# Branch B's inverse rms by halves of the queries, with the pieces of the phases set anew

## The chip, the cores and the metric

The kernel runs on one core of a Trainium2 chip. The metric is the device time of one execution in microseconds; lower is better. Engines are called as in the profile: PE (TensorE, matmuls), PEld (its weight loads), DVE (VectorE), ACT (ScalarE), POOL (GpSimd) and SP (SyncE, which here issues every DMA).

## The reference

One encoder layer is applied to two request groups ("prompt" and "sample") of 1024 tokens and 1024 channels that share the weights. Everything is float32. For the change, branch B matters: four heads, each with two softmax maps whose difference weighs 128-dimensional values, then an rms norm over each head's 128 values, a gate, and a projection.

```
qb = rms_norm(qb.reshape(B, S, H_B, 2, HEAD_DIM), qn_b)
kb = rms_norm(kb.reshape(B, S, H_B, 2, HEAD_DIM), kn_b)
...
ob = diff_attention(qb, kb, vb, lam)            # (p0 - lam * p1) @ v for each head
ob = rms_norm(ob, subln_g) * (1.0 - lam_init)
ob = ob.reshape(B, S, BR_B) * jax.nn.silu(zb)

pa = jnp.einsum('bse,ed->bsd', oa, w_proj_a)
pb = jnp.einsum('bse,ed->bsd', ob, w_proj_b)
merged = jax.nn.sigmoid(ga) * pa + jax.nn.sigmoid(gb) * pb
out = jnp.einsum('bsd,de->bse', merged, w_out)
return x + gate[:, None, :] * out
```

Branch A is grouped-query attention with 8 query heads; its output `oa` is gated in the same way, without the norm over the head.

## The kernel before, in words

The two groups go one after the other through the same stages: a head (projection of keys and values and of the first queries), attention of branch A in phases 0 and 1 (32 units), attention of branch B in phases 2 to 5 (one phase for each head, four units of 256 queries each, `pr` 0 to 3), the gating and the merge of both branches (lines 1028 to 1109), and the output projection (L1128). Matmuls mostly split each float32 operand into a high and a low part and add three products; that is why each block comes as hh, hl and lh.

**Order.** The kernel is written with a tile framework. Python generators emit the work step by step, and `weave` (line 82) interleaves them: each stream has a number of steps and a lead, and the stream that is least far along, less its lead, goes next. `Z_SHARE`, `ATT_W`, `IN_A`, `Z_A`, `LAST_ATT`, `GATED_A`, `FIRST_A` and the like are these numbers and leads for each group and phase. `BEHIND` says how many units the value matmuls of a branch B unit come after its scores; `A_WAIT` how many steps a branch A unit waits ahead of its values. What is emitted first has priority, attention steps more (`AHEAD`, `TRAIN`); a planner then puts each engine's instructions in one fixed order by when its model of time says that they are ready and have a buffer. So on the chip each engine runs its list in order, and the list is not the order of the code.

**Buffers around the change.** PSUM has three "f" banks (projections, merge sums, transposes, the sums of squares of line 975), two "s" tiles (attention scores; after attention also merge sums, `gbank`), and one "a" bank (values). In SBUF the tag "tab" has two buffers, "row" three, "q" two.

**The inverse rms of branch B.** `b_values` (line 937) ends a unit: the value matmuls (L953) fill the a bank; ACT squares it (L968), DVE copies it out (L969), SP sends it to DRAM (L971, `od`); two small matmul pairs against a column of ones sum the squares of 256 queries (L975); DVE copies the two columns into `ss`, a tile of 128 partitions by 4 heads by 8 query tiles (L977). After the last unit of a head (`pr == 3`) POOL computes, over all 8 columns, `(ss + su * su * 2 * HD * EPS) ** -0.5` (L980 to L983); `su` is the first softmax's sum, by which the values have not been divided.

`gated_gen(st, i, hf, oT)` (line 1028) makes the gated inputs of the merge: `i` is a pair of 128-channel blocks (0 and 1 are branch A, 2 and 3 are heads 0, 1 and 2, 3 of branch B), `hf` one half of the queries (512). For `i > 1` and `hf == 0` it transposes the inverse rms of both heads and all queries on PE (L1041, 128x16), copies it out on ACT (L1043) and sends it to DRAM in one write (L1044). Then for each half and each of the two blocks it reads the output and the gate (L1055, L1056) and the row of inverse rms, spread over 128 partitions (L1063), multiplies (L1064, L1068 on DVE) and splits the product into its high part (L1069, ACT) and low part (L1070, DVE).

`merge_gen` (line 1075) multiplies these with the projection weights (L1097): sixteen sums of 12 matmuls for branch A, then sixteen for branch B, in the order of half of the output, half of the queries, block. Of the 12, six take block pair 2 and six pair 3. DVE takes the sums out with the gates (L1108 for A; L1103, L1104, L1106 for B, with ACT at L1105).

In the last attention phase `weave` mixes attention, `fill` (what is left of the gate projections, then 14 or 11 merge sums of branch A) and the gating of pairs 0 to 2; then come the rest of merge A with pair 3's first half, and merge B with its second half.

The code of the functions that the change touches, with the profile's line numbers:

Of the kernel before, what the change touches and what calls it, by code (L numbers as in the profile page):

```python
# [12 lines left out]
F32 = mybir.dt.float32  # L13
# [7 lines left out]
P = 128  # L21
# [3 lines left out]
NTT = T // P  # L25
# [10 lines left out]

Z_SHARE = (
    (8, 21, 4, 2, 4, 3),
    (13, 12, 5, 3, 2, 6),
)  # L40
Z_HEAD = (7, 6)
Z_HEAD_A = (-0.3, -0.32)
ATT_W = (
    (0.825, 1.067, 1.068, 1.192, 1.03, 1.769),
    (1.154, 1.862, 1.041, 1.271, 0.783, 1.144),
)
IN_A = (
    (0.32, -0.07, 0.7, 0.05, 0.25, 0.15),
    (0.1, -0.05, 0.33, 0.3, -0.03, 0.55),
)  # L50
Z_A = (
    (0.2, 0.05, 0.12, -0.05, -0.1, -0.05),
    (0.03, 0.07, 0.2, 0.15, -0.3, -0.1),
)
LAST_ATT = (47, 41)
LAST_FILL = (22, 23)
GATED_A = (0.1, -0.15)
LATE_A = 0.95
QUARTER_P = 200
KV_STEPS = 12  # L60
GATE_AT = 9
FIRST_ATT = 15
FIRST_A = 0.26
TAIL = (2, 5)
TAIL_A = (1.15, 1.2)
LAG = 2
Z_FIRST = (9, 8)
Z_FIRST_A = (-0.05, -0.05)

CUTS = (3, 6)  # L70

BEHIND = 1.4
BEHIND_A = 1.4
AHEAD = 100
PV_LAG = 2
A_WAIT = 1
TRAIN = 200

WHOLE = (True, True)
# [31 lines left out]
def kernel(ctx: ExitStack, tc: tile.TileContext, t: dict):  # L111
# [825 lines left out]
    def b_values(u):  # L937
        acc = ps_a.tile([P, 512], F32, tag="a", name=nm("a"))[:, :256]
        ready = []
        def pv(cc, th, tl):  # L940
            for c in range(2):
                k = cc * 2 + c
                for s, rt in ((0, th), (0, tl), (1, th)):
                    nc.tensor.matmul(
                        acc, u["v"][:, k, s, :], rt[:, c, :],
                        start=(k == 0 and s == 0 and rt is th), stop=(k == 7 and s == 1),
                    )

        if WHOLE[u["h"] // 2]:
            pT = u["pT"].bitcast(F32).rearrange("p (q c b) -> p c q b", q=8, c=8)  # L950
            yield 1
            for k in range(NCH):
                nc.tensor.matmul(acc, u["v"][:, k], pT[:, k], start=(k == 0), stop=(k == 7))  # L953
                if k % 2:
                    yield 1
        else:
            for piece in pT_pieces(u):
                ready.append(piece)
                if len(ready) > PV_LAG:
                    pv(*ready.pop(0))  # L960
                yield 1
            while len(ready) > 1:
                pv(*ready.pop(0))
                yield 1
            pv(*ready.pop())
        sq = mtile("at", [P, 256], bufs=1)
        o = mtile("oo", [P, 256])
        nc.scalar.activation(query_order(sq), piece_order(acc), AF.Square)  # L968
        nc.vector.tensor_copy(query_order(o), piece_order(acc))  # L969
        pr = u["pr"]  # L970
        dma(u["od"][pr // 2][:, (pr % 2) * 256 : (pr % 2 + 1) * 256], o)  # L971
        yield 1
        ps = fbank()
        for i in range(2):
            nc.tensor.matmul(ps[:, i : i + 1], sq[:, i * P : (i + 1) * P], ones_c, start=True, stop=True)  # L975
        ss = u["ss"][:, u["h"]]
        nc.vector.tensor_copy(ss[:, pr * 2 : pr * 2 + 2], ps[:, 0:2])  # L977
        if pr == 3:
            su = u["su"]
            nc.gpsimd.tensor_tensor(out=su, in0=su, in1=su, op=ALU.mult)  # L980
            nc.gpsimd.tensor_scalar(out=su, in0=su, scalar1=2.0 * HD * EPS, scalar2=1.0, op0=ALU.mult, op1=ALU.mult)
            nc.gpsimd.tensor_tensor(out=ss, in0=ss, in1=su, op=ALU.add)
            nc.gpsimd.tensor_tensor(out=ss, in0=ss, in1=nhalf[:, :NTT], op=ALU.pow)  # L983
        yield 1

    def attention(units, feed):
# [41 lines left out]
    def gated_gen(st, i, hf, oT):  # L1028

        if i == 0 and hf == 0:  # L1030
# [4 lines left out]
            row = rtile()[:64, :P]  # L1035
            nc.scalar.activation(row, ps, AF.Copy, scale=0.5)
            dma(st["rA"], row)
        if i > 1 and hf == 0:
            ss = st["ssB"][:, 2 * i - 4 : 2 * i - 2].rearrange("p j n -> p (j n)")
            ps = fbank()[:16, :P]  # L1040
            nc.tensor.transpose(ps, ss, ident)  # L1041
            row = rtile()[:16, :P]
            nc.scalar.activation(row, ps, AF.Copy)  # L1043
            dma(st["rB"][i - 2], row)  # L1044
        rA = st["rA"].rearrange("(j h n) p -> j h (n p)", j=8, h=2)
        rB = st["rB"][i % 2].rearrange("(j h n) p -> j h (n p)", j=2, h=2)
        u = utile().rearrange("p (c s n) -> p c s n", c=2, s=2)
        oT.append(u)
        if i == 3:
# [2 lines left out]
        for c in range(2):  # L1052
# [5 lines left out]
            if e < 4:  # L1058
                for a in range(2):
                    dma(rb[a * 64 : a * 64 + 64], rA[2 * e + a, hf].partition_broadcast(64))  # L1060
                nc.vector.tensor_tensor(out=o, in0=o, in1=z, op=ALU.mult)
            else:
                dma(rb, rB[e % 2, hf].partition_broadcast(P))  # L1063
                nc.vector.scalar_tensor_tensor(  # L1064
                    out=o, in0=o, scalar=subg, in1=z,
                    op0=ALU.mult, op1=ALU.mult,
                )
# [96 lines left out]
    def new_state(g):  # L1164
# [3 lines left out]
        st["rsA"] = const.tile([P, 2, NTT, 4], F32, tag="rsA", name=nm("rsA"), bufs=1)  # L1168
        st["qkb"]["rs"] = const.tile([P, 4, NTT, 4], F32, tag="rsB", name=nm("rsB"), bufs=1)
        st["rA"] = dpool.tile([64, P], F32, name=nm("rA"))  # L1170
        st["rB"] = [dpool.tile([16, P], F32, name=nm("rB")) for _ in range(2)]
        st["od"] = [
            [dpool.tile([P, 512], F32, name=nm("od")) for _ in range(2)] for _ in range(8)
        ]
# [171 lines left out]
```

## Time and profile before

| what | us |
|---|---|
| time, median of 3 runs (lowest to highest) | 1900.5 (1896.01 to 1902.73) |
| span of the profiled execution | 1894.9 |
| own time of the profiled execution | not given beside its span |
| PE busy | 1849.3 |
| DVE busy | 1231.4 |
| ACT busy | 850.1 |
| POOL busy | 366.5 |
| mean granted TensorE clock | 0.993 |

Busy time is the time that an engine spends in instructions; a matmul's end is modelled, so a busy PE may still start its matmuls slowly. In a timeline row stand the start, the duration, the engine and line, the operation, output and inputs, the shapes and the count; in brackets the idle time ahead of it and what ended it. `SPq` is a DMA being issued by SP, not its transfer.

### The profile page before, as it was taken

Reading aid. Unit: us, or ns where it says so; the run is one execution under the profiler, and the core shown is the slowest. Engines: PE = TensorE matmul, PEld = TensorE weight load, DVE = VectorE, ACT = ScalarE, POOL = GpSimd, SP = SyncE. Lnnn points to the kernel's source line nnn. Section 1 sums busy time; section 2 is a strip of 40 time slices with the busy share of each in tenths; the row PEclk is TensorE's granted clock in tenths of the full one; section 3 lists DMA queues with packets and bytes.
Section 4 is the critical chain, followed back from the end, with each engine's and each line's share of the span. In section 5 each row is a group of like instructions: output and inputs, shape, how many; then the busy total and the mean of one; then the engine's idle time right before and its main releaser. Section 6 shows DMA issues by size and latency. Waiting matters only on the chain.

```text
span 1894.9 us, 31953 instructions
## 1 busy us (share of the span) xinstructions
PE 1849.3 (98%) x11430; PEld 1590.8 (84%) x11430; DVE 1231.4 (65%) x1904; ACT 850.1 (45%) x1807; POOL 366.5 (19%) x686
## 2 busy tenths in 40 slices
PE   6899999999999999999999999999999999999999
PEld 4778888888888898787889888888888999877887
DVE  4766766455487667868365777656548776787731
ACT  3544545344455455524223455545446555552310
POOL 0442100011235241010124211000133423300000
PEclk9999999999999999999999999999999999999999
DMA  9135677664355346887551466766625344579532
GB/s 320 59 85 146 162 196 191 170 164 135 100 148 158 93 106 164 248 273 226 193 167 46 123 179 182 197 179 175 168 67 133 102 109 121 135 235 294 189 106 78
DMA packets 277628, 299.54 MB, mean 158 GB/s; under 512 B 37664, under 2 KB 228320, under 8 KB 277472
## 3 DMA queue, kind: packets, MB, share of 16 engines
q1 hardware_dynamic: 277472, 297.51, 55.5%
q8 instruction: 92, 1.51, 0.3%
q14 instruction: 64, 0.52, 0.1%
HBM read 137.91 MB, written 42.04 MB: 95 GB/s over the span
## 4 chain that ended last, share of the span: by engine, by line
PE 82%; DMA 6%; DVE 5%; SPq 3%; ACT 2%; issue 1%; POOL 0%; DVEq 0%; ACTq 0%
PE f L824 23%; PE f L613 20%; PE a L927 6%; PE f L1128 6%; PE s L851 5%; PE s L852 5%; PE a L953 4%; PE f L1097 4%; PE s L1128 3%; PE s L1097 2%; SPq L901 2%; PE s L107 1%; PE f L673 1%; DMA p<-zd 1%; DMA row<-zd 1%
## 5 line engine op out<-in xcount | busy, mean ns | idle before, releaser
L824 PE MATMUL f<-u,w 128*128 128x512 f32 x2184 | 552.9, 394 | 1.7 <-ACT w L206 0.7
L824 PEld LDWEIGHTS f<-u,w 128*128 128x128 f32 x2184 | 401.1, 188 | 81.4 <-ACT w L206 0.9
L613 PE MATMUL f<-w,u 128*128 128x256 f32 x3264 | 449.9, 286 | 2.3 <-DVE u L107 1.5
L613 PEld LDWEIGHTS f<-w,u 128*128 128x128 f32 x3264 | 425.1, 191 | 24.0 <-issue 3.8
L853 DVE TENSOR_REDUCE m<-s 128x1 f32<-128x1024 f32 x256 | 309.7, 1218 | 145.1 <-PE s L852 142.5
L896 DVE STREAM_TRANSPOSE p<-p 128x1024 f32<-128x1024 f32 x192 | 238.3, 1242 | 54.6 <-ACT p L855 49.6
L852 PE MATMUL s<-u,sw 128*128 128x512 f32 x512 | 203.1, 398 | 0.0
L207 DVE TENSOR_TENSOR w<-st,w 128x512 fp32r<-128x512 f32 x188 | 126.3, 704 | 80.8 <-ACT w L206 80.6
L206 ACT ACTIVATE w<-st 128x512 fp32r<-128x512 f32 x188 | 108.9, 625 | 143.2 <-DMA st<-in_w_in_dram 63.7
L855 ACT ACTIVATE p<-s,m,rsB 128x1024 f32<-128x1024 f32 x128 | 154.2, 1205 | 5.2 <-DVE p L895 1.6
L855 ACT ACTIVATE p<-s,m,rsA 128x1024 f32<-128x1024 f32 x128 | 154.4, 1206 | 4.0
L1097 PE MATMUL f<-u,w 128*128 128x512 f32 x576 | 142.3, 397 | 8.6 <-ACT u L1069 3.4
L638 POOL TENSOR_TENSOR rsB<-ss,nhalf 128x4 f32<-128x4 f32 x64 | 66.9, 1045 | 413.8 <-DVE ss L637 404.4
L1097 PEld LDWEIGHTS f<-u,w 128*128 128x128 f32 x576 | 108.9, 190 | 33.6 <-ACT u L1069 3.8
L953 PE MATMUL a<-q,u 128*128 128x256 f32 x512 | 124.6, 379 | 0.8 <-DMA row<-zd 0.7
L927 PE MATMUL a<-q,u 128*64 128x128 f32 x2048 | 123.6, 275 | 0.8 <-DMA q<-p 0.7
L927 PEld LDWEIGHTS a<-q,u 128*64 128x64 f32 x2048 | 112.5, 137 | 12.0 <-issue 7.0
L676 DVE TENSOR_TENSOR u<-f,u 64x256 fp32r<-64x256 f32 (+1 forms) x208 | 84.2, 407 | 50.0 <-ACT u L675 44.7
L851 PE MATMUL s<-u 128*128 128x512 f32 x256 | 109.6, 428 | 3.0 <-ACT p L855 2.9
L1128 PE MATMUL f<-u,w 128*128 128x512 f32 x480 | 111.2, 389 | 0.0
L852 PEld LDWEIGHTS s<-u,sw 128*128 128x128 f32 x512 | 97.0, 189 | 16.1
L953 PEld LDWEIGHTS a<-q,u 128*128 128x128 f32 x512 | 94.1, 190 | 15.2 <-issue 2.3
(195 smaller groups left out, 2101.2 us busy)
## 6 DMA issues: line engine op xcount, KB each, us to landing
q<-p SPq DMA_DIRECT2D x768, 128.0 KB, 2.8
st<-in_w_in_dram SPq DMA_DIRECT2D x128, 256.0 KB, 3.3
zd<-ev SPq DMA_DIRECT2D x96, 256.0 KB, 2.7
sw<-u SPq DMA_DIRECT2D x256, 64.0 KB, 2.1
p<-zd SPq DMA_DIRECT2D x64, 256.0 KB, 4.6
u<-in_w_ada_dram SPq DMA_DIRECT2D x16, 512.0 KB, 8.9
od<-oo SPq DMA_DIRECT2D x64, 128.0 KB, 2.6
st<-in_w_in_dram SPq DMA_DIRECT2D x64, 128.0 KB, 2.8
```

What stands on the lines that cost most here:

```text
L207: nc.vector.tensor_tensor(out=wl, in0=st, in1=wh.bitcast(F32), op=ALU.subtract)
L613: nc.tensor.matmul(ps, lt[c][:, sl], w[c][:, wi, :], start=(k == 0), stop=(k == 23))
L824: nc.tensor.matmul(ps, w[c][:, wi, e * P : (e + 1) * P], rt[c], start=(k == 0), stop=(k == 23),)
L851: nc.tensor.matmul(s[:, sl], q, k[:, sl], start=True, stop=False)
L852: nc.tensor.matmul(s[:, sl], sw, k[:, sl], start=False, stop=True)
L853: nc.vector.tensor_reduce(out=m, in_=s, axis=AX.X, op=ALU.max, negate=True)
L855: nc.scalar.activation(pt.rearrange("p (j c a) -> p j c a", j=4, c=8), s.rearrange("p (c a j) -> p j c a", c=8, j=4), AF.Exp, scale=rs, bi ...
L896: nc.vector.transpose(pt, pt)
L927: nc.tensor.matmul(acc[e * 64 : e * 64 + 64, n * P : n * P + P], u["v"](k), blocks[n][:, e, k], start=(k == 0 and n == 1), stop=(k == 7 an ...
L953: nc.tensor.matmul(acc, u["v"][:, k], pT[:, k], start=(k == 0), stop=(k == 7))
L1097: nc.tensor.matmul(ps, w[:, c, wi, d * P : (d + 1) * P], o[:, oi, :], start=(k == 0), stop=(k == 11))
L1128: nc.tensor.matmul(ps, w[c][:, wi, e * P : (e + 1) * P], m[:, mi, :], start=(k == 0), stop=(k == 23))
```

## The change

`b_values` computes the inverse rms after every second unit (`pr` 1 and 3), over 4 columns each time, not after the fourth over 8. `gated_gen` transposes, for each half of the queries separately, the 4 columns of each of the two heads into one bank, copies both out with one ACT instruction and sends them to DRAM tiles of their own, one for each pair and half; the broadcast reads take them from there. Beside it some twenty of the constants that steer `weave`, the priorities and the lags have other values.

```
--- before.py
+++ after.py
 Z_SHARE = (
     (8, 21, 4, 2, 4, 3),
-    (13, 12, 5, 3, 2, 6),
+    (13, 12, 5, 3, 2, 7),
 )
 Z_HEAD = (7, 6)
-Z_HEAD_A = (-0.3, -0.32)
+Z_HEAD_A = (-0.3, -0.164)
 ATT_W = (
-    (0.825, 1.067, 1.068, 1.192, 1.03, 1.769),
-    (1.154, 1.862, 1.041, 1.271, 0.783, 1.144),
+    (0.652, 1.067, 1.068, 1.192, 1.03, 1.769),
+    (1.154, 2.037, 1.041, 1.271, 0.776, 1.144),
 )
 IN_A = (
-    (0.32, -0.07, 0.7, 0.05, 0.25, 0.15),
-    (0.1, -0.05, 0.33, 0.3, -0.03, 0.55),
+    (0.32, -0.047, 0.7, 0.05, 0.25, 0.15),
+    (0.006, -0.05, 0.529, 0.3, -0.03, 0.55),
 )
 Z_A = (
     (0.2, 0.05, 0.12, -0.05, -0.1, -0.05),
-    (0.03, 0.07, 0.2, 0.15, -0.3, -0.1),
+    (0.166, 0.068, 0.2, 0.15, -0.352, -0.1),
 )
-LAST_ATT = (47, 41)
+LAST_ATT = (45, 42)
 LAST_FILL = (22, 23)
-GATED_A = (0.1, -0.15)
-LATE_A = 0.95
-QUARTER_P = 200
+GATED_A = (0.262, -0.222)
+LATE_A = 0.747
+QUARTER_P = 198
...
-FIRST_ATT = 15
-FIRST_A = 0.26
+FIRST_ATT = 16
+FIRST_A = -0.113
 TAIL = (2, 5)
-TAIL_A = (1.15, 1.2)
+TAIL_A = (1.109, 1.2)
 LAG = 2
 Z_FIRST = (9, 8)
-Z_FIRST_A = (-0.05, -0.05)
+Z_FIRST_A = (0.001, -0.257)
...
-BEHIND = 1.4
+BEHIND = 1.298
...
-A_WAIT = 1
+A_WAIT = 2
...
@@ b_values
         nc.vector.tensor_copy(ss[:, pr * 2 : pr * 2 + 2], ps[:, 0:2])
-        if pr == 3:
-            su = u["su"]
+        if pr % 2:
+            part = slice(pr * 2 - 2, pr * 2 + 2)
+            su, ss = u["su"][:, part], ss[:, part]
             nc.gpsimd.tensor_tensor(out=su, in0=su, in1=su, op=ALU.mult)
             nc.gpsimd.tensor_scalar(out=su, in0=su, scalar1=2.0 * HD * EPS, scalar2=1.0, op0=ALU.mult, op1=ALU.mult)
             nc.gpsimd.tensor_tensor(out=ss, in0=ss, in1=su, op=ALU.add)
-            nc.gpsimd.tensor_tensor(out=ss, in0=ss, in1=nhalf[:, :NTT], op=ALU.pow)
+            nc.gpsimd.tensor_tensor(out=ss, in0=ss, in1=nhalf[:, :4], op=ALU.pow)
@@ gated_gen
-        if i > 1 and hf == 0:
-            ss = st["ssB"][:, 2 * i - 4 : 2 * i - 2].rearrange("p j n -> p (j n)")
-            ps = fbank()[:16, :P]
-            nc.tensor.transpose(ps, ss, ident)
-            row = rtile()[:16, :P]
-            nc.scalar.activation(row, ps, AF.Copy)
-            dma(st["rB"][i - 2], row)
+        if i > 1:
+            bank = fbank()
+            row = rtile()
+            for j in range(2):
+                r = st["ssB"][:, 2 * i - 4 + j, hf * 4 : hf * 4 + 4]
+                nc.tensor.transpose(bank[:4, j * P : (j + 1) * P], r, ident)
+            nc.scalar.activation(row[:4, : 2 * P], bank[:4, : 2 * P], AF.Copy)
+            dma(st["rB"][i - 2, hf].rearrange("j n p -> n j p"), row[:4, : 2 * P].rearrange("n (j p) -> n j p", j=2))
...
-        rB = st["rB"][i % 2].rearrange("(j h n) p -> j h (n p)", j=2, h=2)
...
-                dma(rb, rB[e % 2, hf].partition_broadcast(P))
+                dma(rb, st["rB"][i - 2, hf][c].rearrange("n p -> (n p)").partition_broadcast(P))
@@ new_state
-        st["rB"] = [dpool.tile([16, P], F32, name=nm("rB")) for _ in range(2)]
+        st["rB"] = {(i, hf): dpool.tile([2, 4, P], F32, name=nm("rB")) for i in range(2) for hf in range(2)}
```

## The prediction

> **What bounds the kernel now.** I read the page first, then busy time by stretches, then the waits of TensorE (PE), and last the timeline at the end of the first request group's attention.
>
> ```profile
> span 1894.9 us, 31953 instructions
> PE 1849.3 (98%) x11430; PEld 1590.8 (84%) x11430; DVE 1231.4 (65%) x1904; ACT 850.1 (45%) x1807; POOL 366.5 (19%) x686
> ```
>
> PE is busy for 98% of the span. The shown median of 1900.5 us lies 5.6 above this span; no other time of the profiled execution is given, so the sum is made against 1894.9 and its difference carried to 1900.5. About 0.3% (5.7 us) is what a measurement of this kernel can tell from no change, so faster begins below 1894.8 and slower above 1906.2. PE's idle time, 45.6 us, is all that a change of order can take, besides stretches at a lower granted clock. By stretches of the span (time, PE, PEld, DVE, ACT and POOL busy, then the granted clock, DMA share, GB/s):
>
> ```profile
> 20.00:125.00 105.00, 92.32 (x566) 77.24 (x567) 71.39 (x170) 49.16 (x115) 29.79 (x49) 0.93 0.45 135
> 520.00:775.00 255.00, 251.13 (x1496) 217.55 (x1495) 189.69 (x294) 136.54 (x298) 87.93 (x184) 0.99 0.52 140
> 775.00:870.00 95.00, 88.23 (x381) 70.96 (x381) 72.08 (x108) 34.53 (x65) 6.29 (x9) 0.96 0.87 266
> 1690.00:1765.00 75.00, 70.56 (x314) 57.22 (x313) 51.96 (x77) 23.04 (x45) 4.51 (x7) 1.00 0.82 258
> ```
>
> The idle time sits in the head of the first group (12.7 us), in its middle (3.9), and in the two stretches where attention ends and the merge begins (6.8 and 4.4). The last two hold what the new inverse rms touches. Who made PE wait there (total us, times, longest):
>
> ```profile
> PE f L1097 <- ACT u L1069: 3.4, 1, 3.4
> PE f L1097 <- DVE ssB L977: 2.0, 1, 2.0
> PE f L1097 <- ACT row L1043: 1.4, 1, 1.4
> PE f L1041 <- POOL ssB L983: 0.6, 1, 0.6
> PE s L1097 <- ACT u L1069: 0.6, 1, 0.6
> PE f L673 <- POOL row L662: 0.4, 2, 0.2
> ```
>
> L1097 is the merge matmul, L1069 the split of a gated branch-B tile, L1041 the transpose of the inverse rms. The timeline shows why the 3.4 us arise (start, duration, engine, line, what):
>
> ```profile
> 843.84 0.15 DVE L977 COPY ssB<-f 128x2 f32<-128x2 f32 x1
> 844.42 1.65 POOL L983 TENSOR_TENSOR ssB<-ssB,nhalf 128x8 f32<-128x8 f32 x1
> 846.13 0.28 PE L1041 MATMUL f<-ident,ssB 128*16 128x128 f32 x1 [0.65 <-POOL ssB L983]
> 846.16 7.08 PE L1097 MATMUL f<-u,w 128*128 128x512 f32 x30
> 846.44 0.27 ACT L1043 ACTIVATE row<-f 16x128 f32<-16x128 f32 x1 [7.88 <-PE f L1041]
> 846.74 0.32 SPq L1044 DMA_DIRECT2D rB<-row  x1
> 849.82 0.86 SPq L1063 DMA_DIRECT2D tab<-rB  x2
> 855.23 0.69 DVE L1068 TENSOR_TENSOR q<-tab,q 128x512 f32<-128x512 f32 x1 [4.07 <-DMA tab<-rB]
> 855.95 0.63 ACT L1069 ACTIVATE u<-q 128x512 fp32r<-128x512 f32 x1 [5.08 <-DVE q L1068]
> 856.64 0.79 PE L1097 MATMUL f<-u,w 128*128 128x512 f32 x1 [3.40 <-ACT u L1069]
> 860.34 2.19 PE L1097 MATMUL f<-u,w 128*128 128x512 f32 x5
> 865.59 2.20 PE L1097 MATMUL f<-u,w 128*128 128x512 f32 x9
> ```
>
> One serial chain: last sum of squares at 843.84, power, transpose, copy, a write to DRAM, a broadcast read back, multiply, split, and the first merge matmul that needs it at 856.64: 12.8 us, of which 8.5 (846.74 to 855.23) are the two DMAs. PE has 30 matmuls to cover it. The merge of branch B takes six matmuls from head pair 2 and six from pair 3, so 30 are five half-finished sums, one in each of three f and two s banks; then PE has neither a bank nor an operand. After the wait matmuls start more slowly: 5 in 2.19 us at 860.34, 9 in 2.20 at 865.59. The clock column says why:
>
> ```profile
> 853.00:857.00 4.00, 0.60 (x3) 0.36 (x2) 1.29 (x2) 0.63 (x1) 0.00 (x0) 0.80 0.89 283
> 857.00:861.00 4.00, 4.00 (x10) 2.84 (x10) 3.23 (x5) 1.26 (x2) 0.00 (x0) 0.50 0.90 264
> 861.00:865.00 4.00, 4.00 (x16) 3.20 (x16) 2.71 (x6) 1.26 (x2) 0.00 (x0) 0.84 0.91 315
> ```
>
> If the clock is either 1.0 or 0.5, a mean of 0.84 over 4 us holds 1.3 us at half, so half clock lasts until about 862.3. From 856.64 that is 5.7 us at half speed, a loss of 2.8.
>
> **The change part by part.** *First half freed, group one.* In the old code both halves of the queries need all four units of the head, because one power over 128x8 follows the last unit. In the new one the first half's 128x4 is complete after the second unit, so its transposes, its write and its two reads can all run while the last two units are still on PE. Its gated tiles then stand ready before 845.5, and PE meets no wait when the first merge is over. What is late next is the second half, whose chain is the old one, from 843.84 to about 856. Its cover is the whole first-half block of branch B, 4 sums of 12 matmuls, at 7.08/30 = 0.236 us each 11.3 us, from 845.5 (the end of merge A: 846.13 less the wait of 0.65) to 856.8, and then up to 30 matmuls of half-finished sums of the second half, 7.1 us, to 863.9. So the cover has some 8 us to spare. If it were gone, the 3.40 would stand again. Removed: 0.65 + 3.40 + 2.8 = 6.85; I leave 0.55 for a DVE that is dense there. Term: -6.3.
>
> *Group two.* There the same chain ends in small waits only:
>
> ```profile
> 1703.01 5.74 PE L1097 MATMUL f<-u,w 128*128 128x512 f32 x24 [1.38 <-ACT row L1043]
> 1761.13 0.51 PE L1097 MATMUL s<-u,w 128*128 128x512 f32 x1 [0.62 <-ACT u L1069]
> 1761.77 1.46 PEld L1097 LDWEIGHTS f<-u,w 128*128 128x128 f32 x7 [0.46 <-DVE u L1108]
> ```
>
> The wait at 1761.13 goes, and I count the 0.46 of the weight load behind it with it: -1.0 (bounds 0 and -1.1).
>
> *Transposes.* Four (one for head pair and group) become sixteen, of 4 columns instead of 16. The row at 846.13 has the next matmul start 0.03 us after it; its own duration is 0.28. Twelve more cost +0.4 to +3.4. I take +0.4, since the next start is what PE loses.
>
> *Banks.* Each transpose borrows one of three f banks until ACT copies it out, and ACT works in order:
>
> ```profile
> 782.79 0.27 PE L1041 MATMUL f<-ident,ssB 128*16 128x128 f32 x1
> 785.04 2.35 PE L1097 MATMUL f<-u,w 128*128 128x512 f32 x9 [1.99 <-DVE ssB L977]
> 795.52 0.27 ACT L1043 ACTIVATE row<-f 16x128 f32<-16x128 f32 x1 [0.81 <-issue]
> ```
>
> Held from 782.79 to 795.52, 12.7 us, and in that hold PE ran dry for 1.99; in group two another such hold cost 1.38 (1703.01). Both belong to head pair 2, amid attention. The change has four banks in place of two for each group, and three of them amid attention, so four more such holds than now. Bounds: none of them meets a dry PE (0), or each costs the mean of the two, 1.7 (+6.8). I take one, +1.7, since ACT's copy at 846.44 shows that a hold may also be 0.3 us.
>
> *POOL, ACT and SP.* The four POOL steps of a head become eight:
>
> ```profile
> L638 POOL TENSOR_TENSOR rsB<-ss,nhalf 128x4 f32<-128x4 f32 x64 | 66.9, 1045 | 413.8 <-DVE ss L637 404.4 <-DVE r L882 9.3
> L982 POOL TENSOR_TENSOR ssB<-ssB,suB 128x8 f32<-128x8 f32 x8 | 2.6, 325 | 67.8 <-DVE ssB L977 67.8
> ```
>
> A 128x4 power takes 1.045 us against 1.65 for 128x8; two of them make +0.44 a head, and the last chain gets 0.6 shorter. The small steps double. The added wait is that of L982 for DVE's copy, 67.8/8 = 8.5 us each, now twice as often; behind it on POOL are the rotary steps of the next head and the steps of the softmax factor. Whoever waits for those in the end is PE at L673, 0.4 us in all. Bounds 0 and +0.4; I take 0, because the rows are transposed two tiles late. The copies on ACT (two more for each group, 0.27 each) lie beside an ACT that had been idle 7.88. On SP each new write is followed by reads that wait for its landing, and loads of gate values queue behind them; at 849.82 that order held SP some 3 us and PE was waiting for u, not for a gate. Amid attention the transposed probabilities go through the same queue, so the bounds are 0 and +3 for each of four, and I take 0.
>
> *Pieces of the phases set anew.* Some twenty constants alter which stream gets the next step, so waits disappear and others arise. No row shows the new order. What there is to take is the 12.7 + 3.9 us idle in the head and the middle, and low clock, as here:
>
> ```profile
> 628.00:632.00 4.00, 2.08 (x12) 1.38 (x5) 3.94 (x7) 3.76 (x7) 1.71 (x5) 0.77 0.15 42
> 783.00:787.00 4.00, 2.01 (x10) 1.61 (x10) 4.00 (x6) 1.59 (x3) 0.00 (x0) 1.00 0.92 279
> 630.32 0.79 PE L851 MATMUL s<-u 128*128 128x512 f32 x1 [1.93 <-ACT p L855]
> ```
>
> Bounds: -12 (most of the 16.6) and +6 (three new waits like the 1.93). I take -3.3, a fifth of 16.6, since waits exist to be taken and the order was bad at just those places; this is the softest term.
>
> A wait has a second price. Around the one of 1.93 us the clock fell to 0.77; around the one of 1.99 at 785.04 it stayed at 1.00. So a wait of two microseconds costs itself and, in one case of these two, up to 1.7 us more (3.4 us at half). The Trainium skill, "TensorE: Matmul & The Clock Gate", section "HAM oscillation — how this bites in real kernels", says that idle gaps beyond about 3.4 us send PE to half rate. The trace agrees for the wait of 3.40 and for that of 1.99, not for that of 1.93, which the rule would let pass at full clock. By the rule the bank term is just its wait, +1.7; by the row at 628.00 it can reach +3.4. I keep +1.7 and leave the rest to the range.
>
> **Sum**: -6.3 - 1.0 + 0.4 + 1.7 - 3.3 = -8.5, so 1892.0.
>
> **The rivals.** (1) *Bank holds eat it.* All four extra holds cost 1.7 (+6.8 in place of +1.7) and the pieces bring nothing: -6.3 - 1.0 + 0.4 + 6.8 = -0.1, 1900.4. For it: both holds amid attention cost something. Against: the hold at 846.13 was short. (2) *The first half does not come early.* PE's program may have its transposes behind the 192 matmuls of merge A, as the old one stands at 846.13; then the chain starts there as before and only the 0.65 and some 0.9 go: -1.5 - 1.0 + 0.4 + 1.7 - 3.3 = -3.7, 1896.8. Against: the old transpose has 30 matmuls behind it that were ready as early, so order in the code doesn't bind it. (3) *Overlapping holds: slower.* The halves of one head pair are transposed close together; two of three f banks are gone for 12.7 us, and PE works with one: 12 matmuls (2.8 us), then a wait of 2.0 for its eviction, so 12.7/4.8 = 2.6 waits, 5.3 us, and a half-clock stretch of 3.4 us (4 us at 0.77, and what follows), 1.7 more: 7.0 an overlap. Three overlaps (pair 2 in both groups, pair 3's first half with pair 2's second in one) give 21.0 in place of 1.7: -8.5 - 1.7 + 21.0 = +10.8, 1911.3. Two give 1904.3, so it decides from the third on. Against: it needs ACT late at each of them. (4) *The pieces take their whole bound*: -8.5 - 8.7 = -17.2, 1883.3.
>
> **How the numbers follow.** Forecast 0.50 (its own range 1887 to 1898, from the bounds of banks and pieces), (4) 0.11, (1) 0.17, (2) 0.09, (3) 0.13. Faster by over 0.3%: 0.50 + 0.11 = 0.61; within: 0.17 + 0.09 = 0.26; slower: 0.13. The range 1882 to 1904 takes in (1), (2) and (4) and leaves out most of (3).
>
> **What would show it.** Right: no wait of L1097 for L1069 above 1 us in either group, the clock at 1.00 where merge B begins, reads of the first half's inverse rms issued before the last unit's copy, eight transposes for each group, POOL powers of 128x4. Bank term: waits of L1097 for ACT at the copy of the row, or for DVE L977, at 2 to 9 us in total. Pieces: idle in the first 125 us and between 520 and 775. The prediction is wrong if the wait at the start of merge B stands, or if it goes and PE's idle time turns up as much elsewhere.

## The result, and the profile after

The changed kernel took 1914.6 us (median of 6 runs, 1911.4 to 1921.1), the kernel before 1899.6 beside it (6 runs, 1896.0 to 1902.7): the ratio is 1.0084, with a 95% interval of 1.0065 to 1.0103. It is slower by 0.84%; the forecast was 1892.0, and the range ended at 1904. The profiled execution has a span of 1909.7 us, 14.8 more than before.

The head of the page of the changed kernel:

```profile
span 1909.7 us, 32001 instructions
PE 1859.7 (97%) x11442; PEld 1594.8 (84%) x11442; DVE 1229.8 (64%) x1904; ACT 849.3 (44%) x1811; POOL 387.6 (20%) x718
```

PE runs the twelve extra transposes and nothing else that is new, yet it is busy 10.4 us longer and idle 4.4 us longer (50.0 for 45.6). DVE and ACT do no more than before. POOL is busy 21.1 us longer; 16.8 of that are the four steps of the inverse rms (42.2 for 25.4 us), and PE waits directly for POOL at one line only (L673). So the loss is mostly in order and pace, not in work. The same stretches as in the prediction, and one of the second group, which the last row gives for the kernel before (time, PE, PEld, DVE, ACT and POOL busy, granted clock, DMA share, GB/s):

```profile
20.00:125.00 105.00, 93.58 (x564) 78.19 (x565) 72.22 (x171) 50.80 (x118) 30.89 (x50) 0.93 0.45 135
520.00:775.00 255.00, 246.89 (x1490) 213.13 (x1489) 191.40 (x296) 138.12 (x303) 93.68 (x201) 1.00 0.50 137
775.00:870.00 95.00, 90.02 (x385) 73.17 (x386) 65.13 (x95) 32.32 (x65) 9.24 (x14) 0.95 0.80 250
1500.00:1690.00 190.00, 187.93 (x1098) 166.50 (x1097) 135.58 (x199) 101.15 (x220) 63.89 (x129) 0.99 0.45 122
1690.00:1765.00 75.00, 72.81 (x323) 59.53 (x322) 56.12 (x83) 26.98 (x53) 9.66 (x13) 0.98 0.86 274
```

```profile
1500.00:1690.00 190.00, 189.45 (x1096) 167.94 (x1096) 141.13 (x206) 103.97 (x224) 55.21 (x114) 1.00 0.51 139
```

Where attention ends and the merge begins, PE's idle time did shrink (5.0 for 6.8 us, 2.2 for 4.4). It grew in the middle of the first group (8.1 for 3.9) and in the second group's branch B (2.1 for 0.6). The work in these stretches is up to 15 us late in the changed kernel, so they are a first hint only. Who made PE wait over the whole run (total us, times, longest):

```profile
PE s L851 <- ACT p L855: 3.9, 7, 1.2
PE f L673 <- POOL row L662: 3.4, 3, 1.9
PE a L953 <- DMA q<-p: 2.3, 2, 1.3
PE f L1098 <- ACT u L1070: 2.2, 1, 2.2
PE f L1098 <- DVE u L1109: 1.8, 2, 1.1
PE f L1044 <- DVE ssB L977: 1.8, 1, 1.8
PE s L1098 <- ACT u L1070: 1.7, 2, 1.0
```

(Lines behind L978 stand one to three lines later than before: L1044 are the transposes, L1070 the split, L1098 the merge matmul.) The wait that the change was to remove, L1098 for L1070, stands at 2.2 in place of 3.4 us, and with the s banks the two rows make 3.9 where they made 4.0. The timeline at the start of merge B in the first group shows why:

```profile
854.05 0.38 PE L1044 MATMUL f<-ident,ssB 128*4 128x128 f32 x2
854.47 0.37 ACT L1045 ACTIVATE row<-f 4x256 f32<-4x256 f32 x1 [5.93 <-PE f L1044]
855.38 0.29 SPq L1046 DMA_DIRECT2D rB<-row  x1
856.61 0.16 DVE L977 COPY ssB<-f 128x2 f32<-128x2 f32 x1
858.12 0.80 SPq L1064 DMA_DIRECT2D tab<-rB  x2
861.70 0.69 DVE L1069 TENSOR_TENSOR q<-tab,q 128x512 f32<-128x512 f32 x1 [3.09 <-DMA tab<-rB]
862.42 0.63 ACT L1070 ACTIVATE u<-q 128x512 fp32r<-128x512 f32 x1 [2.83 <-DVE q L1069]
863.11 0.74 PE L1098 MATMUL f<-u,w 128*128 128x512 f32 x1 [2.22 <-ACT u L1070]
864.07 3.85 PE L1098 MATMUL f<-u,w 128*128 128x512 f32 x11
```

The transposes of the first half stand at 854.05, behind 189 of merge A's 192 matmuls, only 2.6 us ahead of the copy of the last sums of squares (856.61). Their numbers had been ready since the head's second unit. From 855.38 on the chain is the old one: a write, a read, a multiply, a split, and PE waits and restarts slowly (11 matmuls in 3.85 us). The prediction named this wait, if it stood, as the sign that it is wrong.

**A count by stage.** A wait is only part of a loss, since slow starts count as busy. So I took the starts of all PE instructions from the trace, cut the span at marks of the program (the value matmuls of certain units, the end of merge A, the end of merge B, the last output matmul of a group), and took from each stage the time that its instructions need where PE is dense: 0.227 us for a matmul of 128x512, 0.120 for 128x256 (0.216 for the values of branch B), 0.057 for the values of branch A, about 0.11 for the small ones. What is left was lost. "Last units" are the last six of branch B's sixteen; "merge" goes from there to the group's end. In us, one profiled execution each (single executions of the kernel before spread over some 9 us, so a difference of 2 says little; two executions stand far from their kernel's median, that of `pair3` 5.5 us above it and that of `halves_setz` 6.7 below):

```
                      group one                group two
kernel           start  last units  merge  start  last units  merge    all
before            57.8      4.8      7.3     8.0      4.0      3.4    85.2
changed           59.8     11.9      6.1    13.5      4.2      3.3    98.7
halves            57.9     13.3      2.4     8.0      7.0      2.3    91.0
pieces            59.8     15.8      2.4    14.9      5.0      1.8    99.7
halves_early      59.4     14.0      0.9     7.8      7.2      0.2    89.5
after_early       58.7     15.6      0.1    15.1      7.8      0.1    97.3
pair3             62.4      6.8      5.8     8.1      7.0      3.7    93.7
pair3_early       58.3      7.0      0.6     7.4      6.5      0.4    80.2
halves_setz       57.5     10.4      2.8     8.0      7.0      2.4    88.2
pieces_last_old   62.2      5.6      5.0    16.8      8.1      1.4    99.0
con_last          57.8     13.0      3.0    11.1      7.4      2.4    94.6
con_att           61.6      5.5      5.8    13.3      8.7      1.4    96.3
con_head          62.5      7.2      6.0     8.1      3.6      2.4    89.9
nudge4            64.0     12.4      4.3     8.5     12.8      0.6   102.5
nudge99           63.0      5.8      5.8     9.4      5.5      2.4    91.9
nudge1            61.7      7.2      7.2     7.7      3.9      2.5    90.3
pair3_early_nudge 65.9     18.6      0.1    10.2      9.9      0.7   105.3
after_nudge       63.7     11.6      5.8    14.6      7.9      1.2   104.8
pair3_early_99    61.5      5.7      0.6     8.1      5.4      0.0    81.3
after_99          63.0     17.8      4.0    15.2      9.8      1.7   111.5
```

The changed kernel lost 13.5 us more than before: 7.1 in the last units of group one, 5.5 in group two ahead of the last units, 2.0 in group one's start, and it won 1.3 in the two merges. The other rows are the experiments.

### The profile page after: what moved, and what is told of

The parts are those of the page before. It is cut to its first block, busy times and chain, and to the rows that moved or that the text cites. A ratio compares the mean times of both kernels' runs of the same rounds, so it can differ in the third digit from the quotient of the medians.

```text
span 1909.7 us, 32001 instructions
## 1 busy us (share of the span) xinstructions
PE 1859.7 (97%) x11442; PEld 1594.8 (84%) x11442; DVE 1229.8 (64%) x1904; ACT 849.3 (44%) x1811; POOL 387.6 (20%) x718
## 4 chain that ended last, share of the span: by engine, by line
PE 77%; DVE 8%; DMA 8%; SPq 3%; ACT 2%; issue 2%; POOL 1%; DVEq 0%; ACTq 0%; POOLq 0%
PE f L824 22%; PE f L613 19%; PE a L927 6%; PE f L1129 6%; PE s L851 5%; PE s L852 5%; PE a L953 4%; PE s L1129 3%; PE f L1098 3%; PE s L1098 2%; DVE m L853 2%; DMA row<-zd 2%; SPq L901 1%; DMA tab<-rB 1%; PE s L107 1%
## 5 line engine op out<-in xcount | busy, mean ns | idle before, releaser
L824 PE MATMUL f<-u,w 128*128 128x512 f32 x2160 | 541.9, 394 | 2.0 <-ACT ev L806 1.1
L1098 PE MATMUL f<-u,w 128*128 128x512 f32 x576 | 142.1, 399 | 4.6 <-ACT u L1070 2.2
L1098 PEld LDWEIGHTS f<-u,w 128*128 128x128 f32 x576 | 109.5, 192 | 30.2 <-DVE u L1109 2.7
L1129 PE MATMUL f<-u,w 128*128 128x512 f32 x480 | 111.2, 389 | 0.0
```

Source lines behind the costliest of these rows:

```text
L824: nc.tensor.matmul(ps, w[c][:, wi, e * P : (e + 1) * P], rt[c], start=(k == 0), stop=(k == 23),)
L1098: nc.tensor.matmul(ps, w[:, c, wi, d * P : (d + 1) * P], o[:, oi, :], start=(k == 0), stop=(k == 11))
L1129: nc.tensor.matmul(ps, w[c][:, wi, e * P : (e + 1) * P], m[:, mi, :], start=(k == 0), stop=(k == 23))
```

## The experiments

All were timed against the kernel before on the same chip; "ratio" is to it, with its 95% interval. The theories: the loss comes from the new inverse rms itself (its place, its banks, what it queues behind), or from the new constants by what they say (C), or from any redrawing of the plan, because the old constants fit the one plan that they make (M). The recorded texts also use P and S for the constants, H for the new inverse rms, and D, Q and R for narrower ones that they explain.

**The change in its two parts.** `halves` has the new inverse rms and every constant of before:

```
-    (0.652, 1.067, 1.068, 1.192, 1.03, 1.769),
+    (0.825, 1.067, 1.068, 1.192, 1.03, 1.769),
...
-A_WAIT = 2
+A_WAIT = 1
```

> The new inverse rms with all the old constants. Theory P (the constants carry the loss): within 3 us of the old kernel's 1899.6, since the first half's transposes still stand behind nearly all of merge A in PE's list and the wait at the start of merge B stays at 2 to 4 us. Rival H (the halves carry it, by banks held and by POOL's extra steps): 1908 or more, with new waits of PE near the transposes.

Measured: 1905.9 us (1902.9 to 1908.8), ratio 1.0036 [1.0023, 1.0049], between the two expectations.

`pieces` has the old inverse rms and every new constant:

```
-        if pr % 2:
+        if pr == 3:
...
-        if i > 1:
+        if i > 1 and hf == 0:
...
```

> The old inverse rms, once per head, with all the new constants. Theory P: 1909 to 1916, as slow as the changed kernel, with lost time in branch A's second phase, near the first transposes amid attention and in the second group's branch B. Rival H: within 3 us of 1899.6.

Measured: 1911.6 us (1908.2 to 1915.7), ratio 1.0067 [1.0055, 1.0080]. Each part alone is slower, and the constants are the larger part. The two excesses, 0.36% and 0.67%, add up to 1.03%, and the whole change has 0.84%. By the table they share a stage: both lose 8 to 11 us in the last units of group one, the two together 7.

**Where the first half is transposed.** The program hands out f banks in the order in which the code asks for them, and `gated_gen` asks for pair 3's first half behind the sums of merge A. `halves_early` and `after_early` ask as soon as the second unit of head 3 has its power:

```
+            if u["h"] == 3 and pr == 1:
+                rows_out(u["st"], 3, 0)      # transposes, copy, write
...
-        if i > 1:
+        if i > 1 and (i, hf) != (3, 0):
```

In `halves_early` the rest is as in `halves`:

> As halves, but the transposes of the third pair's first half (and copy and write) are emitted at once after head 3's second unit, ahead of the rest of attention. Theory P: the wait of the merge for L1069's counterpart and the half clock behind it go in the first group, 5 to 7 us less than halves, 1892 to 1896. Rival: a bank held amid attention, or the second half's chain, takes the place of the wait, and the time is that of halves within 2 us.

Measured: 1903.0 us (1900.5 to 1909.3), ratio 1.0024 [1.0015, 1.0033].

In `after_early` the rest is as in the changed kernel:

> As the changed kernel, with the same early transposes. Theory P: 4 to 6 us less than the changed kernel's 1914.6, so 1908 to 1911: still slower than the old one, because the constants are untouched. If the first half's place in the list is the whole cause of the loss, 1900 or less.

Measured: 1910.5 us (1908.9 to 1911.2), ratio 1.0060 [1.0048, 1.0072]. Both gain on their parent, by 0.12% and 0.24%, which is about the size of the intervals (2.9 us for `halves_early`, where 5 to 7 were expected). The stage shows it clearly: the merges lose 1.1 us in all for the parent's 4.7, and 0.2 for 9.4. Not all of that reaches the total: `after_early` wins 9.2 us there and loses 3.7 of it in group one's last units and 5.2 in group two.

**Only pair 3 by halves.** `pair3` leaves heads 0 and 1 as they were (one power, one transpose, one write, all constants of before) and halves only heads 2 and 3; `pair3_early` also moves the transposes of the first half:

```
-        if pr == 3:
+        if pr == 3 or (u["h"] > 1 and pr == 1):
...
-        if i > 1 and hf == 0:
+        if i == 2 and hf == 0:               # pair 2: one transpose, one write
...
-        if i == 3:                           # pair3
+        if i == 3 and hf == 1:               # pair3_early: the first half is out already
             rows_out(st, hf)
```

> Old constants; heads 0 and 1 as in the old kernel (one power, one transpose, one write for the pair), heads 2 and 3 by halves, the first half transposed right after head 3's second unit. Theory D (the merge wait is freed as predicted, and what eats it is the last attention phase, where pair 2's two halves change the order on DVE and ACT): the loss in that phase falls back towards the old kernel's 4 us and the 6.4 us won at the merge stay: 1892 to 1896. Rival R (any new order of the lists brings its own waits): 1899 to 1905, with a new wait somewhere in the last attention phase.

Measured: 1892.7 us (1890.9 to 1894.9), ratio 0.9963 [0.9951, 0.9975]. This beats both kernels.

> As pair3_early, but the first half of pair 3 is transposed where the changed kernel has it, behind the attention. Theory D: 2 to 5 us more than pair3_early, since the transposes stand behind merge A in PE's list. If they are equal, the place of the transposes is not what frees the merge.

Measured: 1900.7 us (1897.0 to 1906.2), ratio 1.0011 [1.0000, 1.0021]. So the move of the transposes is worth 0.48%, 8.1 us, more than the 2 to 5 that were expected; the merges account for it (1.0 us lost for 9.5). One thing moves with the transposes: emitted in `b_values`, they also get the lead of the attention's steps (`AHEAD`). Whether the earlier bank or the earlier priority frees them, these runs do not separate. In `pair3_early` (L943 copy, L944 write, L1083 multiply, L1084 split, L1112 merge):

```profile
819.81 0.49 SPq L944 DMA_DIRECT2D rB<-row  x1
831.40 0.38 SPq L1078 DMA_DIRECT2D tab<-rB  x1
837.62 0.69 DVE L1083 TENSOR_TENSOR q<-tab,q 128x512 f32<-128x512 f32 x1
842.52 1.14 ACT L1084 ACTIVATE u<-q 128x512 fp32r<-128x512 f32 x2
848.27 2.88 PE L1112 MATMUL f<-u,w 128*128 128x512 f32 x12
852.77 0.36 ACT L943 ACTIVATE row<-f 4x256 f32<-4x256 f32 x1
855.78 6.96 PE L1112 MATMUL f<-u,w 128*128 128x512 f32 x30
```

The write of the first half is issued at 819.81, and the high parts of its two tiles are ready at 843.7, 4.6 us before the row at 848.27, in which merge A ends and merge B begins. The second half's copy at 852.77 has the cover that the prediction counted. The stretch that held 6.8 us of idle time and a mean clock of 0.96 before:

```profile
775.00:870.00 95.00, 90.77 (x406) 73.66 (x405) 74.62 (x112) 34.58 (x67) 8.53 (x13) 1.00 0.87 269
```

406 PE instructions in place of 381 fit into the same 95 us, at full clock.

**A load at the head of DVE's list.** The wait behind the start that costs `halves` most is in the last units:

```profile
807.39 0.75 DVE L1065 SCALAR_TENSOR_TENSOR row<-row,subg,row 128x512 f32<-128x512 f32 x1 [3.77 <-DMA row<-zd]
809.22 1.18 DVE L853 TENSOR_REDUCE m<-s 128x1 f32<-128x1024 f32 x1
810.44 0.30 ACT L854 ACTIVATE m<-m,rsB 128x1 f32<-128x1 f32 x1 [8.55 <-DVE m L853]
812.12 0.79 PE L851 MATMUL s<-u 128*128 128x512 f32 x1 [5.93 <-ACT p L855]
```

DVE's next step is a gating step whose gate tile is still on its way, and behind it in the list stands the row maximum of a softmax. ACT waits 8.55 us for that, PE 5.93 for ACT. `halves_setz` takes the gate loads of pair 2 away; POOL fills the tile with ones, so that part of the gating is left out:

```
-            dma(z, st["zd"][(e, hf)])
+            if i == 2:
+                nc.gpsimd.memset(z, 1.0)
+            else:
+                dma(z, st["zd"][(e, hf)])
```

> As halves, but the gate values of pair 2 (heads 0 and 1) are not loaded: POOL sets that tile to one, so this part of the gating is left out. Theory Q (DVE's list stood 3.8 us before a multiply for the late load of the gate, the row maximum behind it came late, and PE waited 5.9 us for a score buffer and ran at half clock): that wait and the half clock go, 5 to 9 us less than halves' 1905.9, so 1897 to 1901. Rival: the wait comes from the extra transposes or POOL steps themselves, and stays: 1904 to 1907.

Measured: 1907.6 us (1901.0 to 1910.5), ratio 1.0041 [1.0029, 1.0054]: no gain, where 1897 to 1901 was expected. In its profile, of its fastest execution (1901.0), PE's wait for the softmax there is 2.1 us and not 5.9, but the stage still loses 10.4. The load explains that one wait. It is not shown to be the cause of the stage's loss, because without it the plan is another one.

**The constants in groups.** `pieces_last_old` is `pieces` with the four that weigh the last attention phase set back:

```
-LAST_ATT = (45, 42)
+LAST_ATT = (47, 41)
...
-GATED_A = (0.262, -0.222)
+GATED_A = (0.1, -0.15)
...
-TAIL_A = (1.109, 1.2)
+TAIL_A = (1.15, 1.2)
...
-BEHIND = 1.298
+BEHIND = 1.4
```

> As pieces, with the four constants of the last phase and of branch B's lag (LAST_ATT, GATED_A, TAIL_A, BEHIND) as in the old kernel. Theory: the 11 us lost in the first group's last phase, less the 4.5 won at the merge, and the second group's branch B go: 1903 to 1906, the rest being branch A's phases (2.5 and 3 us). If those constants do nothing: 1911.

Measured: 1910.8 us (1908.5 to 1914.0), ratio 1.0061 [1.0048, 1.0073], as slow as `pieces`, where 1903 to 1906 was expected. The stage that these constants steer came back to 5.6 us, but the merges rose from 4.2 to 6.4, and starts and group two took the rest. Then each group alone on the kernel before: `con_last` has just those four new, `con_att` just ATT_W, IN_A, Z_A and Z_SHARE, `con_head` just Z_HEAD_A, FIRST_ATT, FIRST_A, Z_FIRST_A, LATE_A, QUARTER_P and A_WAIT. `nudge4` has no new constant at all, only

```
-AHEAD = 100
+AHEAD = 101
```

> The old kernel with only the four constants of the last phase and of branch B's lag new (LAST_ATT, GATED_A, TAIL_A, BEHIND). Theory S (the stages show it: these move the gating into attention, 11 us lost there, 4.5 won at the merge): 1903 to 1907. Theory M (any change redraws the whole plan, and a plan that isn't chosen for its own waits has more of them; sizes don't add up): anything from 1897 to 1910, with losses also in stages before the last phase.

Measured: 1907.5 us (1903.9 to 1909.4), ratio 1.0046 [1.0034, 1.0058].

> The old kernel with only the constants that mix attention, projections and gates within the phases new (ATT_W, IN_A, Z_A, Z_SHARE). Theory S: the losses of branch A's second phase in group one (2.5) and of group two's phases (2.7 and 3.7 us) come with these: 1905 to 1909. Theory M: 1900 to 1912, with losses in other places than in pieces.

Measured: 1909.8 us (1906.0 to 1913.7), ratio 1.0061 [1.0048, 1.0075].

> The old kernel with only the constants of the heads and branch A's wait new (Z_HEAD_A, FIRST_ATT, FIRST_A, Z_FIRST_A, LATE_A, QUARTER_P, A_WAIT). Theory S: the head loses 0.3 us in pieces, so 1898 to 1901, no change. Theory M: also slower, 1902 to 1908, by waits in later stages.

Measured: 1902.8 us (1901.6 to 1904.7), ratio 1.0025 [1.0015, 1.0035].

> The old kernel with AHEAD, the lead in priority of attention steps, at 101 and not 100, which says nothing by itself but redraws the order of PE's list. Theory S: 1898 to 1900. Theory M: 1900 to 1908, slower by new waits of the same kinds (ACT or DVE held by a late load, PE behind them).

Measured: 1913.4 us (1910.6 to 1915.5), ratio 1.0078 [1.0065, 1.0091]. The three groups cost 0.46 + 0.61 + 0.25 = 1.32% alone and 0.67% together: they don't add. And one step of one priority costs nearly as much as the whole change, more than either theory allowed. Its profile has the same kind of wait as `halves`, at another place, and one for a load of transposed probabilities (the last row):

```profile
783.26 0.69 DVE L1061 TENSOR_TENSOR row<-row,row 128x512 f32<-128x512 f32 x1 [3.18 <-DMA row<-zd]
786.25 0.29 ACT L854 ACTIVATE m<-m,rsB 128x1 f32<-128x1 f32 x1 [7.61 <-DVE m L853]
787.92 0.50 PE L851 MATMUL s<-u 128*128 128x512 f32 x1 [1.97 <-ACT p L855]
801.54 6.68 PE L953 MATMUL a<-q,u 128*128 128x256 f32 x16 [2.98 <-DMA q<-p]
```

**Other draws of the plan.** If M held, any nudge should cost. `nudge99` has AHEAD at 99, `nudge1` one hundredth in one piece (IN_A[0][1] from -0.07 to -0.06); `pair3_early_nudge` and `after_nudge` are those two kernels with AHEAD at 101, `pair3_early_99` and `after_99` with 99.

> The kernel before with AHEAD at 99 in place of 100: the planner weighs its due times by one step less, nothing else differs. If any redrawing of the plan costs, because the constants of before fit the one plan that they make (theory M): slower than before, 1903 to 1915 us. If the draws lie on both sides of before: anywhere from 1890 to 1912 us, with one chance in two of 1900 us or less. If only the constants of the change cost something (theory C): within 3 us of 1899.6 us.

Measured: 1903.1 us (1899.6 to 1907.1), ratio 1.0021 [1.0008, 1.0035].

> The kernel before with one number moved, IN_A[0][1] from -0.07 to -0.06. Theory M: slower than before by 3 to 15 us, 1903 to 1915 us. Theory C: within 3 us of 1899.6 us, as a hundredth of one piece moves at most a few instructions.

Measured: 1900.6 us (1896.4 to 1904.7), ratio 1.0008 [0.9997, 1.0018]. M as a rule fails here: this plan costs nothing that can be measured.

> The kernel with heads 0 and 1 of branch B as before and heads 2 and 3 by halves, pair 3's first half transposed early, and AHEAD at 101 in place of 100. Theory M: the 6.9 us that the early half gave against before stay, and the redrawn plan costs some 14 us, as AHEAD 101 did to the kernel before: 1903 to 1909 us, and 5 to 9 us below 1913.4 us. If the gain of the early half was itself a lucky draw: 1911 to 1916 us.

Measured: 1916.3 us (1912.8 to 1917.7), ratio 1.0095 [1.0081, 1.0109]. The merges lose 0.8 us, as without the nudge, but the last units of group one lose 18.6, more than in any other row. The total is where the rival had it (a lucky draw), above the kernel before with the same nudge (1.0078): in this plan the early half is worth nothing in all, though it keeps the merges short.

> The changed kernel with AHEAD at 101 in place of 100. Theory M (the new constants do not fit better than any draw): anywhere between 1903 and 1918 us, as likely below 1914.6 us as above. Theory C (the new constants mean something and were set for this plan): slower than 1914.6 us by 3 to 14 us, 1918 to 1928 us.

Measured: 1915.1 us (1913.6 to 1919.9), ratio 1.0095 [1.0081, 1.0109].

> The kernel with heads 0 and 1 of branch B as before and heads 2 and 3 by halves, pair 3's first half transposed early, with AHEAD at 99 in place of 100. If what the merge gains adds to what the plan of AHEAD 99 costs (1903.1 us without the early half): 1894 to 1898 us. If the early half is itself a redrawing whose cost cannot be foreseen: anywhere between 1893 and 1916 us, most likely above 1900 us; the merge's own share (6 to 8 us less lost from the start of merge B on in both groups) stays in either case.

Measured: 1895.8 us (1891.7 to 1899.9), ratio 0.9987 [0.9975, 0.9999]; here the gain adds to the plan's cost (0.9987 against 1.0021 without it).

> The changed kernel with AHEAD at 99 in place of 100. If the new constants cost by the place that they happen to give to steps: anywhere from 1900 to 1918 us. If they cost in every plan: 1912 to 1918 us, as with AHEAD 100 and 101 (1914.6 and 1915.1 us).

Measured: 1924.8 us (1917.2 to 1929.9), ratio 1.0137 [1.0112, 1.0163], slower than either expectation. Ratios by AHEAD 99, 100, 101: before 1.0021, 1, 1.0078; `pair3_early` 0.9987, 0.9963, 1.0095; changed 1.0137, 1.0084, 1.0095. The changed kernel is the slower one against before in all three plans, by 1.16, 0.84 and 0.17% (the last within the intervals), which speaks against one unlucky plan. Three plans are few, though: a plan alone moves each of these kernels by 0.5 to 1.3%. In `after_99` the last units of group one hold this:

```profile
793.39 0.69 DVE L1062 TENSOR_TENSOR row<-row,row 128x512 f32<-128x512 f32 x1 [4.07 <-DMA row<-zd]
798.14 0.15 DVE L977 COPY ssB<-f 128x2 f32<-128x2 f32 x1
798.34 1.22 PE L1098 MATMUL f<-u,w 128*128 128x512 f32 x2 [7.97 <-DVE ssB L977]
```

The gate load at the head of DVE's list holds the list for 4.07 us, and five more steps come before the copy of the sums of squares; until then the f bank stays taken, and PE is dry for 7.97 us. A second of the three f banks is held by transposes all that time, from 774.33 until ACT copies them out at 803.52:

```profile
774.33 0.38 PE L1044 MATMUL f<-ident,ssB 128*4 128x128 f32 x2
803.52 0.36 ACT L1045 ACTIVATE row<-f 4x256 f32<-4x256 f32 x1
```

## Why the prediction was wrong

**The step that failed first** is "so its transposes, its write and its two reads can all run while the last two units are still on PE". They could by their data, but the kernel puts them elsewhere. What came is rival (2), which had 0.09: the transposes stand behind merge A. I dismissed it because the old transpose at 846.13 has thirty ready matmuls behind it; but that one stood behind 192 others all the same. `pair3` against `pair3_early` shows it: 0.48% for the place of two transposes in the code. That it is their bank, asked for late and so given late, is my reading; no run shows it apart from their priority. The -7.3 for both groups was too small, if anything. With the early place the merges lose 0.2 to 1.1 us in all five kernels that have it, whatever the plan, against 10.7 before (-9.6 to -10.5). The changed kernel got -1.3 there, `halves` -6.0 and `pieces` -6.5 without it, so its own worth depends on the parent: 3.6 us for `halves`, 8.5 and 9.2 for `pair3` and the changed kernel.

**Pieces of the phases set anew, -3.3**, was the larger miss in size: alone they measured +0.67%, 12.7 us, and my upper bound was +6. The bound took three new waits from one row, and the sign came from "waits exist to be taken and the order was bad at just those places", which is no reading of a row. Two stages carry it. Group two up to the last units lost 8.0 us before; it loses 13.3 to 16.8 in every kernel that has the new ATT_W, IN_A, Z_A and Z_SHARE (seven of them), and 7.4 to 11.1 in all others. `con_att`, which has nothing else new, is one of them. That much is a cost of those constants in every plan tried. One of the waits there in the changed kernel, and the clock behind it:

```profile
1532.05 0.65 POOL L981 TENSOR_TENSOR suB<-suB 128x4 f32<-128x4 f32 x1
1534.86 0.19 POOL L982 TENSOR_SCALAR suB<-suB 128x4 f32<-128x4 f32 x1
1535.51 0.62 PE L673 MATMUL f<-ident,row 128*128 128x128 f32 x2 [1.94 <-POOL row L662]
```

```profile
1535.00:1539.00 4.00, 3.49 (x10) 2.82 (x11) 3.88 (x8) 2.96 (x7) 1.89 (x4) 0.58 0.32 89
```

Two steps of the inverse rms stand in POOL's list ahead of the one that PE waits for. `pieces` has the same wait without them, 1.33 us, and its clock stays at 1.00 there. `con_att` has no such wait (0.2 us) and loses 13.3 all the same, so this one is not what these constants cost in general.

The last units of group one lose 4.8 to 7.2 in nine kernels and 10.4 to 18.6 in the other eleven; with `con_last` alone it is 13.0, with the new inverse rms alone 13.3, with AHEAD 101 alone 12.4. The mechanism seen in three of them (`halves`, `nudge4`, `after_99`) is the in-order list of DVE with a gating step at its head that waits for a load. Why these plans put it there, and the others don't, stays open: my test by `halves_setz` didn't answer it.

**Heads 0 and 1 by halves** had no price of their own beside banks and queues. `halves_early` and `pair3_early` differ in just that, and by ratio it costs 0.61% (1.0024 against 0.9963); in the table 7.0 us of it is in the last units of group one. With the late place, `halves` against `pair3`, it costs 0.25%. Whether it costs anything in other plans wasn't tried, and a plan alone moves a kernel by as much.

**Banks, +1.7.** In the changed kernel waits for L977 are 1.8 at L1044 and 0.4 more at a merge matmul, less than the 2.0 and 1.4 that before had, so as a sum of waits the term was too high there. But the 1.75 at the new transposes opens a cluster of three waits that ends in half clock, 7.7 us by the last section, while the 2.0 of before stayed at full clock; that cluster is most of the 11.9 us lost in the last units. What share of it is the bank's, no run shows. The holds are long: 20.5 us (771.55 to ACT's copy at 792.01) and 12.5 for pair 2 in group one. `after_99` with 7.97 shows the mechanism of rival (3), two of three banks taken. That rival's 1911.3 lies near the result, but by luck: no three overlapping holds of 7.0 us are in the changed kernel, whose waits for L977 come to 2.2.

**Transposes +0.4 and POOL 0** were right in the durations of a transpose and of a power:

```profile
L984 POOL TENSOR_TENSOR ssB<-ssB,nhalf 128x4 f32<-128x4 f32 x16 | 17.5, 1094 | 1.1
L1044 PE MATMUL f<-ident,ssB 128*4 128x128 f32 x16 | 3.2, 271 | 1.8 <-DVE ssB L977 1.8
```

The waits of L673 for POOL rose from 0.4 to 3.4 us, but they stand at 2.7 in `pieces`, which has POOL's old steps, and at 0.4 in `halves`: they come with the constants, and steps of the inverse rms stand ahead of one of them (above). The +0.44 a head counted the powers alone; all four steps of a head cost 2.1 us more.

**What stays open.** Whether the new constants cost the same in plans further away, and what in ATT_W, IN_A, Z_A or Z_SHARE makes group two slower. M as a rule is refuted (`nudge1`), C alone can't explain `nudge4`; the runs support a real cost of the constants on top of a spread of plans of its own size.

## What to carry to other kernels

A value that is ready early is used early only if every step of its chain is asked for early: look in the code for what stands ahead of its transpose, which takes a PSUM bank and a place in PE's list. When an automatic planner orders a nearly full engine, time a change with a few meaningless nudges of both kernels beside it, and read its worth from the stage that it touches: here a single step of a priority moved the total by 0.8%, while the merges lost 0.2 to 1.1 us in all five kernels with the early place. Each of the three groups of new constants cost something here (0.25 to 0.61%); forecast no gain from such numbers unless a row shows one.

## What the runs showed of the hardware

Short waits cost more than their length. In the changed kernel three waits within 6 us, none above 1.75, were followed by half clock:

```profile
771.55 0.38 PE L1044 MATMUL f<-ident,ssB 128*4 128x128 f32 x2 [1.75 <-DVE ssB L977]
773.14 0.50 PE L851 MATMUL s<-u 128*128 128x512 f32 x1 [1.21 <-ACT p L855]
775.64 6.47 PE L953 MATMUL a<-q,u 128*128 128x256 f32 x16 [1.30 <-DMA q<-p]
```

```profile
772.00:776.00 4.00, 1.56 (x5) 1.06 (x6) 3.47 (x7) 3.69 (x8) 1.51 (x3) 0.81 0.80 212
776.00:780.00 4.00, 4.00 (x10) 3.15 (x10) 2.75 (x3) 0.57 (x1) 0.00 (x0) 0.50 0.93 264
780.00:784.00 4.00, 4.00 (x16) 3.27 (x15) 3.75 (x5) 2.41 (x6) 0.00 (x0) 0.84 1.02 295
861.00:865.00 4.00, 1.89 (x5) 1.51 (x6) 3.30 (x6) 1.52 (x3) 0.00 (x0) 0.77 0.64 221
865.00:869.00 4.00, 4.00 (x16) 3.22 (x15) 1.70 (x3) 0.63 (x1) 0.00 (x0) 0.80 0.73 187
```

If the clock is 1.0 or 0.5, the first three rows hold 1.5 + 4.0 + 1.3 = 6.8 us at half, a loss of 3.4 on top of 4.3 us of waits. The last two, around the single wait of 2.22 at 863.11, hold 1.8 + 1.6 = 3.4 us, a loss of 1.7. The Trainium skill, "TensorE: Matmul & The Clock Gate", section "HAM oscillation — how this bites in real kernels", says that gaps beyond about 3.4 us bring half rate. Here a gap of 2.22 us did, and a cluster of shorter ones did.

The clock records of the traces say what counts. In them the clock is 1.0 or 0.5 and changes only at the ends of pieces of 3.41 us on a fixed grid; the 3.4 and 6.8 us above are one piece and two. I cut the twenty traces into these pieces, from 30 us on. Of the pieces at full clock, all 53 in which PE was idle for over 55% were followed by one at half, and none of the 10530 with under 30%; in between it was 58 of 185. So watch how much idle time falls into one piece, and not the longest gap. The wait of 2.22 us lies whole in one (65% idle). The 1.99 us at 785.04 in the kernel before fell on two (20% and 38% idle), and the clock stayed at 1.00.
